# A hybrid decoder layer on one core: output projection by seven products, roots by Ln and Exp, reordered border loads

## The chip, the cores and the metric

The kernel runs on one core of a Trainium2 chip. The core has TensorE (PE: matmuls from SBUF into PSUM), VectorE (DVE), ScalarE (ACT), GpSimd (POOL) and SyncE (SP, which issues the DMAs here). Each takes its instructions in order and waits on semaphores for the others. The metric is device time in microseconds, the median of several executions.

## The reference

One layer over 4096 tokens of width 1024. A norm and one input projection feed three mixers: a chunked gMLP (256 columns), a gated recurrence (256) and eight heads of forgetting attention (512). Their gated outputs y are projected, added to x, and normed again.

```
h = _rmsnorm(x, norm_g[layer])
proj = jnp.einsum('bsd,de->bse', h, w_in[layer])
...
y = jnp.concatenate([y_a, y_b, y_c], axis=-1)
x = x + jnp.einsum('bse,ed->bsd', y, w_out[layer])
...
return _rmsnorm(x, final_norm_g)
```

The norm is x · rsqrt(mean(x²) + 1e-6) · g. All is float32.

## The kernel before

To keep float32's accuracy every large product is made of three: each operand is split into a part that TensorE's fast float32 form holds (`hi`) and the rest (`lo`), and hi·hi, hi·lo and lo·hi are summed in PSUM.

The work comes in three stages. *Projection* (0 to about 1650 us) norms x (`xprep`, `xnorm`), transposes it and makes all columns; the gMLP (`gm_v`) and the recurrence (`hgrn`) run between its products. *Attention* (to 3031 us) walks 32 units, a unit being a pair of heads and a block of 512 queries. For each key tile `do_tile` makes scores `st` and their exponentials `pt`; `do_accs` sums `pt` for the denominators on DVE and POOL; `do_pv` multiplies by the values; `finish_unit` makes the denominators' product `pl`, normalizes and stores to `d_yc`. It is a generator, and `tick(fin)` moves it on by one step. Row maxima of units ahead (`rowmax`, products `sm`, maxima `mp`) run between. A unit's keys (`ka`, `kb`), queries (`qa`, `qb`, `qc`) and values come by DMA in the order in which the program issues them on SP; at the border between the stages `unit_load`, `load_next` and `load_qb` set this order. U0 = 3 units have their maxima made in the projection.

*Output projection* (`out_tile`, from 3031 us) goes over 32 tiles of 128 tokens. A tile has two halves of 512 columns; a half is 8 depth slices × 3 products = 24 matmuls of 128x512 into one PSUM tile `o` (L1588). DVE adds it to the x tile (L1592), ACT squares and sums (L1594); a tick later the root (`rsqrt_small`, L93) and the scaling by the final gain (L1600) follow, and SP stores the tile. `y_load` fetches y for 256 tokens (a block, 16 of them), `y_split` makes hi and lo. The x tiles take three buffers, `qb0` to `qb2`, in turn. w_out is loaded and split during attention (`load_wo`).

`rsqrt_small` makes 1/sqrt on DVE alone, from a bit trick and three Newton steps: 11 operations on 128x1 or 128x4 values, used for all norms.

## Time and profile before

| | us |
|---|---|
| median of 3 runs | 3394.76 (3393.18 to 3395.24) |
| the profiled execution | 3389.97 |
| its span | 3388.1 |
| PE busy | 3264.9 |
| DVE, ACT, POOL busy | 2337.5, 1615.7, 1383.7 |
| output projection, first to last matmul's start | 3031.33 to 3379.40 |

The span is the time from the first to the last instruction of the profiled execution. A row of the table of waits reads "engine, its instruction and line, the engine and instruction that ended the wait: total us, number of waits, the longest". A row of a group reads "line, engine, operation, out<-in, shapes, count | busy us, mean ns | idle time before it and what ended it". A row of the timeline begins with start and duration in us. A matmul's end is modelled, so the distance between starts is its cost.

### The profile page before, as it was taken

The numbers are of one execution on the slowest core, as the hardware profiler recorded it, in microseconds if no ns is written. First come the engines' busy times: TensorE is split into PE (matmuls) and PEld (weight loads), VectorE is DVE, ScalarE is ACT, GpSimd is POOL, SyncE is SP. The second block draws the span as 40 slices with busy tenths as digits, with TensorE's granted clock in tenths as the row PEclk, the third lists the DMA queues.
The fourth block names the chain that finished last, engine by engine and source line by source line (L and its number), as shares of the span: only waits on it lengthen the run. The fifth ranks groups of instructions, "written<-read, shape, count | busy, mean of one in ns | idle before, by whom it ended". The sixth has DMA issues, their size and how long they took to land.

```text
span 3388.1 us, 54808 instructions
## 1 busy us (share of the span) xinstructions
PE 3264.9 (96%) x20314; PEld 2401.5 (71%) x20314; DVE 2337.5 (69%) x4521; ACT 1615.7 (48%) x2979; POOL 1383.7 (41%) x1504
## 2 busy tenths in 40 slices
PE   7999999999999999989899999999999999999999
PEld 7888787978888788777655555555555555558887
DVE  5467745686466845687388888888888888665554
ACT  5435553355434543355255555555555555552221
POOL 2134312342223321344265666666666676660000
PEclk9999999999999999989899999999999999999999
DMA  4432243213342133312550142014201411014443
GB/s 152 138 101 70 70 130 123 94 60 113 114 128 76 51 98 102 104 57 63 123 133 25 35 129 63 26 35 126 66 26 35 116 54 35 27 59 146 148 144 112
DMA packets 204898, 297.06 MB, mean 88 GB/s; under 512 B 19588, under 2 KB 127252, under 8 KB 204630
## 3 DMA queue, kind: packets, MB, share of 16 engines
q1 hardware_dynamic: 204630, 293.56, 28.7%
q8 instruction: 159, 2.61, 0.3%
q14 instruction: 109, 0.89, 0.1%
HBM read 208.83 MB, written 84.43 MB: 87 GB/s over the span
## 4 chain that ended last, share of the span: by engine, by line
PE 53%; DVE 10%; issue 1%; POOL 1%; ACT 1%; DMA 0%; SPq 0%; DVEq 0%; POOLq 0%; ACTq 0%
PE pv L1371 12%; PE o L1588 10%; PE st L1485 7%; PE acc L953 7%; PE sm L149 7%; PE st L1488 6%; DVE mp L162 3%; DVE acc L1354 2%; PE acc L989 2%; PE pl L1311 1%; DVE wlo L249 1%; POOL acc L1354 0%; DVE sm L157 0%; DVE rn L1318 0%; DVE xq L545 0%
## 5 line engine op out<-in xcount | busy, mean ns | idle before, releaser
L1492 ACT ACTIVATE pt<-st,bias 128x512 f32<-128x512 f32 (+3 forms) x1152 | 705.9, 651 | 530.4 <-PE st L1488 431.5
L1354 POOL TENSOR_TENSOR acc<-acc,pt 128x512 f32<-128x512 f32 (+2 forms) x516 | 635.1, 1231 | 316.4 <-PE st L1485 224.4
L162 DVE TENSOR_REDUCE mp<-sm 128x2 f32<-128x1024 f32 (+1 forms) x460 | 536.0, 1192 | 142.9 <-PE sm L149 142.9
L953 PE MATMUL acc<-hhi,whi 128*128 128x512 f32 x1376 | 558.6, 406 | 13.6 <-ACT gu L778 11.1
L953 PE MATMUL acc<-hlo,whi 128*128 128x512 f32 x1376 | 545.3, 396 | 1.3 <-DVE hlo L313 1.3
L953 PE MATMUL acc<-hhi,wlo 128*128 128x512 f32 x1376 | 546.0, 397 | 0.0
L1371 PE MATMUL pv<-pt,v 128*64 128x512 f32 (+3 forms) x2304 | 491.1, 567 | 1.1 <-POOL pt L1497 0.7
L1485 PE MATMUL st<-qa,ka 128*128 128x512 f32 (+2 forms) x1152 | 466.3, 407 | 7.2 <-ACT pt L1492 6.2
L1354 DVE TENSOR_TENSOR acc<-acc,pt 128x512 f32<-128x512 f32 (+2 forms) x516 | 416.2, 807 | 74.8 <-PE pv L1371 34.5
L1488 PE MATMUL st<-qc,kb 68*128 68x512 f32 (+2 forms) x1152 | 441.1, 384 | 3.5 <-DMA qc<-d_m 3.5
L149 PE MATMUL sm<-kb,qb 66*128 66x512 f32 (+2 forms) x1152 | 355.6, 390 | 25.3 <-DVE mp L162 16.1
L1371 PEld LDWEIGHTS pv<-pt,v 128*64 128x64 f32 x2304 | 154.4, 137 | 277.2 <-issue 253.6
L1485 PEld LDWEIGHTS st<-qa,ka 128*128 128x128 f32 x1152 | 219.6, 191 | 179.0 <-issue 96.5
L953 PEld LDWEIGHTS acc<-hhi,whi 128*128 128x128 f32 x1376 | 260.4, 189 | 75.6 <-ACT gu L778 12.5
L249 DVE SCALAR_TENSOR_TENSOR wlo<-wraw,gT,whi 128x256 fp32r<-128x256 f32 (+1 forms) x480 | 255.7, 572 | 75.9 <-ACT whi L248 74.6
L953 PEld LDWEIGHTS acc<-hhi,wlo 128*128 128x128 f32 x1376 | 260.2, 189 | 61.0
L989 PE MATMUL acc<-whi,hhi 128*128 128x256 f32 (+1 forms) x1024 | 295.4, 288 | 7.5 <-ACT FL L996 5.7
L953 PEld LDWEIGHTS acc<-hlo,whi 128*128 128x128 f32 x1376 | 261.0, 190 | 58.0 <-DVE hlo L313 2.3
L989 PE MATMUL acc<-wlo,hhi 128*128 128x256 f32 (+1 forms) x1024 | 289.3, 283 | 0.0
L989 PE MATMUL acc<-whi,hlo 128*128 128x256 f32 (+1 forms) x1024 | 289.1, 282 | 0.0
L149 PEld LDWEIGHTS sm<-kb,qb 66*128 66x128 f32 x1152 | 211.5, 192 | 93.2 <-DVE mp L162 38.2
L1488 PEld LDWEIGHTS st<-qc,kb 68*128 68x128 f32 x1152 | 222.0, 193 | 37.6 <-issue 3.9
(274 smaller groups left out, 4988.4 us busy)
## 6 DMA issues: line engine op xcount, KB each, us to landing
wraw<-in_w_in_dram SPq DMA_DIRECT2D x120, 512.0 KB
x<-in_x_dram SPq DMA_DIRECT2D x88, 512.0 KB
qa<-d_qh SPq DMA_DIRECT2D x64, 256.0 KB
out_dram<-x SPq DMA_DIRECT2D x31, 512.0 KB
kb<-d_kh SPq DMA_DIRECT2D x38, 256.0 KB
d_kh<-chi SPq DMA_DIRECT2D x32, 256.0 KB
d_kl<-clo SPq DMA_DIRECT2D x32, 256.0 KB
d_qh<-chi SPq DMA_DIRECT2D x32, 256.0 KB
```

Source lines behind the costliest of these rows:

```text
L149: nc.tensor.matmul(ps[:, :n], qb[0:66, h, i * P : (i + 1) * P], kb[0:66, h, :n], start=True, stop=True)
L162: nc.vector.tensor_reduce(dst, ps, axis=AX.X, op=ALU.max)
L249: nc.vector.scalar_tensor_tensor(lo[:, k, :n], raw, g, hi[:, k, :n].bitcast(F32), op0=ALU.mult, op1=ALU.subtract)
L953: nc.tensor.matmul(ps, ww[:, k, cs], hh[:, k, :], start=n == 0, stop=n == 3 * KC - 1)
L989: nc.tensor.matmul(o, hh[:, k, ts_], ww[:, k, :width], start=n == 0, stop=n == 3 * KC - 1)
L1311: nc.tensor.matmul(pl[64 * h : 64 * h + 64, :], ones_v, acc[h], start=True, stop=True)
L1354: ins = eng.tensor_tensor(a[:, q0:], src[:, q0:], pts[i][:, q0:], op=ALU.add)
L1371: mm = nc.tensor.matmul(pv[64 * h : 64 * h + 64, q0:], vt[:, i, 64 * h : 64 * h + 64], group[h][i][:, q0:], start=kb == 0, stop=kb == nkb - 1,
L1485: first = nc.tensor.matmul(st[:, qm:], ka_t[g][:, h, cs], qa_t[u % 2][:, h, qm:], start=True, stop=False)
L1488: nc.tensor.matmul(st[:, qm:], kb_t[g][0:68, h, cs], qc_t[u % 2][:, h, qm:], start=False, stop=True)
L1492: nc.scalar.activation(pt[:, q0:], st[:, q0:], AF.Exp, bias=bias_of[u][:, h, kb : kb + 1])
L1588: nc.tensor.matmul(ps, a[:, k % 4, o : o + P], b[k][:, cs], start=n == 0, stop=n == 3 * KC - 1)
```

## The change

**Output projection.** The first NCL = 2 blocks (4 tiles) keep the old form. From block 2 on, `out_block` multiplies the 256 tokens × 1024 by the 1024 × 1024 matrix as 2 × 2 by 2 × 2 blocks with seven products instead of eight. The two token halves and the two depth halves give a11, a12, a21, a22; four combinations s1 to s4 of them are made on POOL (`comb2`). Four combinations of w_out's quarters are made once (`combine`), between the first four tiles, from a second load of w_out. Each of the seven products m0 to m6 is 4 depth slices × 3 = 12 matmuls of 128x512. A product is added by DVE to one or two of the block's four quarters of x; m3 is first added to a copy `u` of m0, which POOL adds to three quarters. m1 and m2 go to the halves of one PSUM tile `ab`, the others to `pr`. While a block is made, the parts (hi by ACT, lo by DVE) for the next ones are made. `norm_out` squares both halves at once.

**Roots.** `rsqrt_small` takes Ln and Exp on ACT and one Newton step on DVE.

**Border.** `load_qb(U0)` is issued before unit 1's loads, and unit 1's entries come first in the list of key tiles to load.

**Denominators.** `finish_unit` moves on twice per eight tiles rather than three times, and waits two yields rather than four before its store.

**w_out.** The raw rows are held for a step, and split by column halves.

```diff
-        nc.vector.tensor_scalar(
-            y.bitcast(I32), v.bitcast(I32), -0.5, 1597463007.0, op0=ALU.mult, op1=ALU.add
-        )
-        for _ in range(3):
-            nc.vector.tensor_tensor(t, y, y, op=ALU.mult)
...
+        nc.scalar.activation(y, ssum, AF.Ln, scale=scale, bias=eps_c)
+        nc.scalar.activation(y, y, AF.Exp, scale=-0.5)
+        nc.vector.tensor_tensor(t, y, y, op=ALU.mult)
+        nc.vector.scalar_tensor_tensor(t, t, -0.5, v, op0=ALU.mult, op1=ALU.mult)
+        nc.vector.scalar_tensor_tensor(y, t, 1.5, y, op0=ALU.add, op1=ALU.mult)
...
-            for _ in range(4):
+            for _ in range(2):
                 yield
             nc.sync.dma_start(d_yc[p][Q], t)
...
         loaded = [0]
+        load_qb(U0)
         if U0 > 1:
             unit_load(1)
             unit_bias(1)
             loaded[0] = 1
+            for e in [e for e in need if e[2] == 1]:
+                need.remove(e)
+                need.appendleft(e)
             while 1 not in ka_t:
                 load_next()
-        load_qb(U0)
...
-                if n in (5, 6, 7):
+                if n in (6, 7):
                     tick(fin)
...
+        def combine(k):
+            raw = [xp.tile([P, D], F32, tag="x", name="wr") for _ in range(2)]
+            for r, kk in zip(raw, (k, k + KH)):
+                nc.sync.dma_start(r, wv[:, kk, :])
+            (b11, b12), (b21, b22) = [(r[:, :512], r[:, 512:]) for r in raw]
...
+            for i, (t, a, b) in enumerate(((t1, b12, b11), (t2, b22, t1), (t3, b22, b12), (t4, b21, t2))):
+                nc.vector.tensor_tensor(t, a, b, op=ALU.subtract)
+                hi, lo = place(4 * k + i)
+                nc.scalar.copy(hi, t)
+                nc.vector.tensor_tensor(lo, t, hi.bitcast(F32), op=ALU.subtract)
...
+            def split(v):
+                pr = big.tile([P, 2, 4, P], F32R, tag="big", name="ya")
+                nc.scalar.copy(pr[:, 0], v)
+                nc.vector.tensor_tensor(pr[:, 1], v, pr[:, 0].bitcast(F32), op=ALU.subtract)
+                parts[t].append(pr)
...
+            plan = [
+                (b11, [x11]), (comb[0], [x12, x22]), (comb[2], [x21, x22]), (comb[1], []),
+                (b22, [x12]), (comb[3], [x21]), (b21, [x11]),
+            ]
+            for m, (b, adds) in enumerate(plan):
+                pr = parts[t][m]
+                ps = ab[:, m - 1] if m in (1, 2) else ps_st.tile([P, 512], F32, tag="st", name="pr")
+                n = 0
+                for k in range(KH):
+                    for i, w in ((0, b[k][0]), (0, b[k][1]), (1, b[k][0])):
+                        nc.tensor.matmul(ps, pr[:, i, k], w, start=n == 0, stop=n == 3 * KH - 1)
+                        n += 1
+                if m == 0:
+                    u = fs.tile([P, 512], F32, tag="rc", name="u", bufs=3)
+                    nc.scalar.copy(u, ps)
+                for xx in adds:
+                    nc.vector.tensor_tensor(xx, ps, xx, op=ALU.add)
+                if m == 3:
+                    nc.vector.tensor_tensor(u, ps, u, op=ALU.add)
+                    for xx in (x22, x21, x12):
+                        nc.gpsimd.tensor_tensor(xx, xx, u, op=ALU.add)
...
+                    xts[t + 1] = [x3_load(2 * t + 2, f"qb{(t + 1 - NCL) % NQB}"), x3_load(2 * t + 3, "")]
```

*DVE in the output stage.* Before, a tile's work is two additions and a root; here from the second scaling of one tile on:

```order
L1600 SCALAR_TENSOR_TENSOR x3_30567<-x3_30567,fry_30719,fgB_29641 128x1024 [waits DVE_49]
L1592 TENSOR_TENSOR x3_30650<-o_30653,x3_30650 128x512 [waits DMAHW5_49,DMAHW4_49,PE_49]
L1592 TENSOR_TENSOR x3_30650<-o_30681,x3_30650 128x512 [waits PE_49]
L1596 TENSOR_TENSOR ss_30652<-ss_30652 128x1 [waits Activation_49]
L99 TENSOR_SCALAR frv_30801<-ss_30652 128x1 [waits DVE_49]
L100 TENSOR_SCALAR fry_30802<-frv_30801 128x1 [waits DVE_49]
L104 TENSOR_TENSOR frt_30803<-fry_30802 128x1 [waits DVE_49]
L105 SCALAR_TENSOR_TENSOR frt_30803<-frt_30803,frv_30801 128x1 [waits DVE_49]
L106 SCALAR_TENSOR_TENSOR fry_30802<-frt_30803,fry_30802 128x1 [waits DVE_49]
```

After, a block in the middle of the stage. x3_30976 is the first tile of its tokens (x11 and x12), x3_30978 the second (x21 and x22); `ya` are lo parts for the blocks ahead; the first row is the last scaling of the block before:

```order
L1624 SCALAR_TENSOR_TENSOR x3_30804<-x3_30804,fry_31116,fgB_29444 128x1024 [waits DVE_49]
L1735 TENSOR_TENSOR x3_30976<-pr_31099,x3_30976 128x512 [waits DMAHW3_49,DMAHW0_49,Activation_49]
L1682 TENSOR_TENSOR ya_31168<-s_31166,ya_31168 128x512 [waits Activation_49]
L1682 TENSOR_TENSOR ya_31190<-s_31188,ya_31190 128x512 [waits PE_49,Activation_49]
L1735 TENSOR_TENSOR x3_30976<-ab_31098,x3_30976 128x512 [waits PE_49]
L1735 TENSOR_TENSOR x3_30978<-ab_31098,x3_30978 128x512
L1682 TENSOR_TENSOR ya_31209<-s_31207,ya_31209 128x512 [waits Activation_49]
L1735 TENSOR_TENSOR x3_30978<-ab_31098,x3_30978 128x512 [waits PE_49]
L1735 TENSOR_TENSOR x3_30978<-ab_31098,x3_30978 128x512 [waits DVE_49]
L1737 TENSOR_TENSOR u_31112<-pr_31171,u_31112 128x512 [waits PE_49]
L1682 TENSOR_TENSOR ya_31247<-yr1_31041,ya_31247 128x512 [waits DMAHW6_49,DMAHW5_49,DMAHW7_49,DMAHW0_49,Activation_49]
L1735 TENSOR_TENSOR x3_30976<-pr_31193,x3_30976 128x512 [waits PE_49,Pool_49]
```

and on to the block's last product and its first root:

```order
L1735 TENSOR_TENSOR x3_30978<-pr_31219,x3_30978 128x512 [waits PE_49]
L1682 TENSOR_TENSOR ya_31317<-s_31315,ya_31317 128x512 [waits Activation_49]
L101 TENSOR_SCALAR frv_31236<-ss_31233 128x1 [waits Activation_49]
L105 TENSOR_TENSOR frt_31238<-fry_31237 128x1 [waits Activation_49]
L106 SCALAR_TENSOR_TENSOR frt_31238<-frt_31238,frv_31236 128x1 [waits DVE_49]
L1735 TENSOR_TENSOR x3_30976<-pr_31250,x3_30976 128x512 [waits PE_49]
L107 SCALAR_TENSOR_TENSOR fry_31237<-frt_31238,fry_31237 128x1 [waits DVE_49]
L1624 SCALAR_TENSOR_TENSOR x3_30978<-x3_30978,fry_31237,fgB_29444 128x1024 [waits DVE_49]
```

The additions of m0 and m1 now stand behind both roots of the block before, m4's behind a wait for POOL, and m6's behind a root's first half, which waits for ACT.

*PE in the output stage.* Before, a tile's first matmul writes a PSUM tile of its own (here the change from one half to the next):

```order
L1588 MATMUL o_30681<-woh_29477,ylo_30547 128x512
L1588 MATMUL o_30737<-woh_29032,yhi_30542 128x512 [waits DVE_49]
L1588 MATMUL o_30737<-wol_29033,yhi_30542 128x512
L1588 MATMUL o_30737<-woh_29032,ylo_30543 128x512
L1588 MATMUL o_30737<-woh_29085,yhi_30542 128x512
```

After, the change from m1 to m2, both in `ab`:

```order
L1729 MATMUL ab_30926<-th_29833,ya_30801 128x512
L1729 MATMUL ab_30926<-tl_29834,ya_30801 128x512
L1729 MATMUL ab_30926<-th_29833,ya_30801 128x512
L1729 MATMUL ab_30926<-th_29552,ya_30824 128x512 [waits DVE_49,Activation_49]
L1729 MATMUL ab_30926<-tl_29553,ya_30824 128x512
L1729 MATMUL ab_30926<-th_29552,ya_30824 128x512
```

The wait for DVE on m2's first row (the last of these) is for the second addition of m1 from the same tile, DVE's row x3_30806<-ab_30926; in the block shown above its like is x3_30978<-ab_31098, ahead of s4's lo part.

*SP at the border.* Before, with `qb` the queries of the next row maxima:

```order
L121 DMA qc_17541<-d_ql_90 64x2x512 [waits DMAHW6_49]
L126 DMA qc_17541<-d_m_130 1x1024 [waits Pool_49]
L126 DMA qc_17541<-d_m_130 1x1024 [waits DMAHW0_49]
L114 DMA kb<-d_kh_66 64x2x512 [waits DMAHW1_49]
L115 DMA kb<-d_cb_114 4x2x512 [waits DMAHW2_49]
L132 DMA ka<-d_kh_66 64x2x512 [waits DMAHW3_49]
L133 DMA ka<-d_kl_74 64x2x512 [waits DMAHW4_49]
L1235 DMA v<-d_v_98 128x4x128 [waits DMAHW5_49]
L1240 DMA qb_17538<-d_qh_84 64x2x512 [waits DMAHW6_49]
L114 DMA kb<-d_kh_67 64x2x512 [waits DMAHW7_49]
```

After:

```order
L1241 DMA qb_17325<-d_qh_84 64x2x512 [waits DMAHW0_49]
L120 DMA qa_17324<-d_qh_82 64x2x512 [waits DMAHW1_49]
L115 DMA kb<-d_kh_68 64x2x512 [waits DMAHW4_49,DMAHW3_49,DMAHW5_49,DMAHW2_49,DMAHW7_49,Activation_49,Pool_49]
L116 DMA kb<-d_cb_116 4x2x512
L115 DMA kb<-d_kh_69 64x2x512
L116 DMA kb<-d_cb_117 4x2x512
L121 DMA qa_17324<-d_qh_82 64x2x512 [waits DMAHW6_49]
L122 DMA qc_17328<-d_ql_90 64x2x512
```

The queries moved from behind unit 1's queries, keys and values to ahead of all of them.

## The prediction

> **What bounds the kernel now.** I read the page first, then PE's waits, then the output stage by itself.

> ```profile
> PE 3264.9 (96%) x20314; PEld 2401.5 (71%) x20314; DVE 2337.5 (69%) x4521; ACT 1615.7 (48%) x2979; POOL 1383.7 (41%) x1504
> 3031.00:3380.00 349.00, 348.79 (x1538) 288.21 (x1536) 175.72 (x498) 76.44 (x157) 3.00 (x3) 1.00 0.38 134
> ...
> PE sm L149 <- DVE mp L162: 16.1, 32, 1.0
> PE acc L953 <- ACT gu L778: 11.1, 6, 3.0
> PE pm L812 <- DVE mp L157: 8.1, 1, 8.1
> PE xtp L306 <- DVE x L291: 8.1, 2, 6.3
> PE sm L149 <- DMA qb<-d_qh: 6.3, 1, 6.3
> PE xtp L306 <- DVE xr1t L105: 6.2, 1, 6.2
> ...
> PE pl L1311 <- DVE acc L1354: 5.9, 4, 2.0
> ...
> PE st L1488 <- DMA qc<-d_m: 3.5, 1, 3.5
> ...
> PE xtp L306 <- DVE xr1t L104: 2.6, 1, 2.6
> ```

> PE is busy for 3264.9 of 3388.1 us, so all its waits together are 123 us, and the time can fall only by fewer products or by some of these small waits. In the output stage (second row) PE is busy for 348.79 of 349 us: nothing else matters there, DVE has half its time free (175.72), ACT more (76.44), and POOL does nothing (3.00). This stage holds the largest edit.

> ```profile
> 3031.33 0.50 PE L1588 MATMUL o<-woh,yhi 128*128 128x512 f32 x1
> ...
> 3379.40 0.39 PE L1588 MATMUL o<-woh,ylo 128*128 128x512 f32 x1
> ...
> L1588 PE MATMUL o<-woh,yhi 128*128 128x512 f32 x512 | 199.3, 389 | 0.0
> L1588 PE MATMUL o<-woh,ylo 128*128 128x512 f32 x512 | 199.2, 389 | 0.0
> L1588 PE MATMUL o<-wol,yhi 128*128 128x512 f32 x512 | 199.2, 389 | 0.0
> ...
> L1592 DVE TENSOR_TENSOR x<-o,x 128x512 f32<-128x512 f32 x64 | 44.1, 690 | 104.8 <-PE o L1588 104.8
> L1600 DVE SCALAR_TENSOR_TENSOR x<-x,fry,fgB 128x1024 f32<-128x1024 f32 (+1 forms) x33 | 41.2, 1252 | 1.1
> ...
> L1564 DVE TENSOR_TENSOR ylo<-yr,yhi 128x1024 fp32r<-128x1024 f32 x29 | 35.5, 1225 | 29.6 <-PE o L1588 27.0 <-ACT yhi L1563 2.6
> ...
> L105 DVE SCALAR_TENSOR_TENSOR frt<-frt,frv 128x1 f32<-128x1 f32 x96 | 15.3, 160 | 3.3
> ...
> L1594 ACT ACTIVATION_READ_ACCUMULATOR junk<-x 128x1 f32 x64 | 11.9, 186 | 0.0
> ```

> The three groups of L1588 have 512 matmuls each, 1536 in all, and begin every (3379.40 − 3031.33)/1535 = 0.2268 us. A tile of 128 tokens has 48 of them, so 256 tokens take 96 × 0.2268 = 21.77 us.

> **The output products.** Four tiles stay as they are: 192 matmuls, 43.5 us. The other 14 blocks of 256 tokens take 7 products of 12 matmuls: 84 × 0.2268 = 19.05 us each, against 21.77. So 14 × 12 = 168 matmuls go, worth 168 × 0.2268 = **38.1 us if PE never waits**. What comes instead lies on DVE, ACT and POOL: per block DVE has nine additions from PSUM at 0.69 (L1592's row), seven lo parts, two final scalings at 1.25 (L1600) and eight small operations at 0.16; POOL has seven additions; ACT seven casts, a copy, two squares and four small functions. On DVE that is some 15 us of 19: by its sum it fits. The order is the trouble. Products m1 and m2 write the two halves of one PSUM tile, `ab`, and the first matmul of m2 waits for DVE's second addition of m1. DVE takes its work in the order of the rows shown with the change, so m2 waits for all that stands ahead of that addition: the last additions and both norms of the block before.

> The trace before has no POOL addition in this stage. The nearest rows are the attention's, where DVE and POOL do the same addition side by side, and the casts of the first stage:

> ```profile
> L1354 POOL TENSOR_TENSOR acc<-acc,pt x516: 448/1286/2146, 1651.5 to 3026.6; 128x512 f32<-128x512 f32 x140, 128x384 f32<-128x384 f32 x24, 128x128 f32<-128x128 f32 x8
> L1354 DVE TENSOR_TENSOR acc<-acc,pt x516: 271/692/1787, 1671.6 to 3030.0; 128x512 f32<-128x512 f32 x140, 128x384 f32<-128x384 f32 x24, 128x128 f32<-128x128 f32 x8
> ...
> L312 ACT CAST hhi<-xtp 128x512 fp32r<-128x512 f32 x64 | 35.6, 586 | 37.0 <-PE xtp L306 37.0
> L265 ACT ACTIVATE junk<-x 128x1024 bf16<-128x1024 f32 x32 | 33.6, 1051 | 5.4 <-DMA x<-in_x_dram 5.4
> ...
> L560 ACT ACTIVATE dec<-z 128x4 f32<-128x4 f32 x16 | 3.3, 206 | 20.4 <-DVE z L471 20.4
> ```

> A POOL addition of 128x512 takes 1.29 us (median). DVE's takes 0.69 by its median and up to 1.79: the same operation is often held up while POOL works. So a lo part (two inputs from SBUF, as this addition) costs 0.69 with POOL quiet and, at a doubling, about 1.35 beside it. [...]

> Now one block, with zero at m2's first matmul and 0.1 us (an estimate, from the 0.04 between the last matmul's modelled end and the addition at 3379.83, plus a start) per step between engines. PE ends m2 at 2.7, m3 at 5.4, m4 at 8.2, m5 at 10.9, m6 at 13.6; the next block's m0 at 16.3 and m1 at 19.05. DVE adds m3 to `u` from 5.5 to 6.2. POOL then adds `u` to three tiles: 3 × 1.29, to 10.2. Only behind the third comes DVE's addition of m4 to x12: 10.3 to 11.0. Two lo parts: 12.4 (13.7 beside POOL). m5's addition: 13.1 (14.4). Square, its read (1.05 + 0.19), Ln and Exp (0.2 each by L560's row): 14.9 (16.3). Two small operations, then m6's addition, which could have begun at 13.7: 16.0 (17.4). First scaling: 17.5 (18.8). The second norm's Square began with the end of m6's addition and its rstd is there at 18.5 (19.9); second scaling: 19.7 (21.2). m0's addition 0.69, two lo parts 1.38, m1's two additions 1.38: 23.2 (24.6). So m2 starts again after **23.3 us with quiet lo parts, 24.7 with contended ones**; I take 24.0, between them, since POOL's four combinations for the next block fall right behind its three adds. Floors: 19.05 if DVE is always in time, 21.7 if the three POOL additions weren't waited for.

> The change of form costs too. Block 2's first x tile is loaded into the buffer that tile 3's output leaves (`qb0`):

> ```profile
> SPq L1579 <- DMA out_dram<-x: 69.0, 29, 3.2
> ```

> Such a load waits up to 3.2 us for the store today, hidden. Counted from the stage's begin, tile 3 ends at 43.5 + about 1.7 (DVE now splits w_out's combinations between the tiles: 8 × 0.69 of extra work per tile ahead of the additions that free PSUM), its norm and issue at 50, the store at 53, the load (512 KB; an estimate of 3.5 to 4 from the store's 3.2) at 57, then five DVE operations of 0.69: block 2's m2 begins at 60.3 where PE alone could at 49. From there 13 steps of 24.0 = 312.0, and the last block's 13.6; the last two blocks prepare no successor, about −3.5. Sum 60.3 + 312.0 + 13.6 − 3.5 = 382.4, against 348.5 before: **+33.9 us**, where the count of matmuls says −38.1.

> **The small edits.** The new root (Ln and Exp on ACT, one Newton step on DVE) takes a chain of 11 small DVE operations to 4 plus 2 on ACT:

> ```profile
> 30.33 0.15 DVE L99 TENSOR_SCALAR xr1v<-xss 128x1 f32<-128x1 f32 x1
> ...
> 34.35 0.75 DVE L291 TENSOR_SCALAR x<-x,rstd 128x1024 f32<-128x1024 f32 x1
> ```

> At the start the last x tile waits 4.0 us in such a chain, of which some 1.1 stay; the transposes that wait for it (6.2 and 2.6 above) come earlier until the next DMA or ACT step binds: −3.0, bounds 0 and −8.8. In the projection the added 0.2 us operations on ACT lie beside PE; the shorter chains may trim the waits of 8.1 (pm) and 11.1 (gu): −2.0, bounds 0 and −8.1. Queries first at the border: PE's 6.3 us on `qb` shrink, but unit 1's loads now stand behind in SP's queue and `qc` (3.5) may be late by as much again: −3.5, bounds −6.3 and +3.5. Denominators a tile later: of 5.9 us on DVE's `acc`, −3.0, bounds 0 and −5.9. w_out's loads and the d_yc store stand beside a busy PE: 0. Sum **−11.5**, bounds −29 and +3.5.

> The tail after the last matmul:

> ```profile
> 3379.83 0.69 DVE L1592 TENSOR_TENSOR x<-o,x 128x512 f32<-128x512 f32 x1 [4.75 <-PE o L1588]
> ...
> 3383.63 1.41 DVE L1600 SCALAR_TENSOR_TENSOR x<-x,fry,fgB 128x512 f32<-128x512 f32 x2
> ```

> DVE's small operations in it get shorter by about 1, the last store is larger again: 0.

> **Sum.** The profiled execution took 3389.97 (span 3388.1 and 1.9 around it), 4.8 below the median of the runs, 3394.76. 3389.97 + 33.9 − 11.5 = 3412.4; on the median's basis 3417.2, which I give as **3417**.

> **Rivals.**
> - *The lock.* Every lo part and small DVE operation that meets POOL waits for its end. The chain from m4's addition to the second scaling then lengthens by about half a POOL addition more, a step of 25.4: 13 × 1.4 = +18, so 3435. For it: the 1.79 us maximum. Against: the median of 0.69 with POOL 41% busy. [...]
> - *Faster by the count.* The wait for `ab` is short because DVE runs ahead: a step of 19.05. It takes 13 × 4.95 = 64 us off and, with block 2 late as above, leaves about 3353; without that, 3345 (−38.1 − 11.5). It decides if DVE gets to m1's additions within 19.05 us of m2's start. Against it: the rows' order, which puts m6 (13.6) ahead of both norms, and from m6's end to m2 at least 7.4 us of DVE against 5.4 of PE.
> - *A small gain.* POOL's three additions don't hold m4's addition: a step of 21.7, 13 × 2.3 = −30: 3387, just faster. It needs POOL additions of under 0.9 us (three from 6.3 on, then m4's addition and two lo parts, all by 11.0); the median row has 1.29.
> - *Only the output edit acts*, and the small ones give nothing: 3429.

> **How the numbers follow.** Forecast (23.3 to 24.7: 3408 to 3426) 0.56, with the last rival 0.10 in the same sign but for its edge; the lock 0.10; the small gain 0.13; the count 0.08; left over, 0.03. A measurement can tell about 0.2% from no change, here 6.8 us. Faster 0.22 (the count, most of the small gain, a little from the rest), same 0.10 (edges of the small gain and of the forecast's low side with the small edits at their best), slower 0.68. The range leaves out the count and little above the lock: 3366 to 3440.

> **What would show it.** Right: in the output stage PE idles some 5 us per block, ended by DVE's x additions, always ahead of m2; DVE's row for the lo parts averages 0.9 to 1.3 us; block starts 24 us apart; one long PE wait near 50 to 60 us after the stage begins. The stage lasts 375 to 400 us and begins about 11 us earlier. Wrong: steps under 21.8, PE waits spread over other products, or a stage that begins later than before.

## The result and the profile after

| | before | after |
|---|---|---|
| median, us | 3393.97 (3389.92 to 3395.24, 4 runs) | 3478.0 (3475.04 to 3480.25, 4 runs) |
| ratio | | 1.0252 (1.0240 to 1.0265) |
| profiled execution, span | 3389.97, 3388.1 | 3478.55, 3476.8 |
| first score product (`st`) begins | 1647.5 | 1641.0 |
| attention, from there to the first `o` | 1383.9 | 1398.2 |
| output stage, first to last matmul's start | 348.1 | 429.1 |

The change is slower by 84 us. I had forecast 3417 and a range to 3440: the sign was right, the size was not. The table, from the timelines of both traces, says where: the projection gains 6.5 us, the attention loses 14.3, and the output stage, with 168 matmuls fewer, takes 81 us more. (The profiled executions differ by 88.6.) In the experiments below, one execution of w_out_only took 11083 us, and its ratio leaves it out. The page of the kernel after:

```profile
PE 3265.4 (94%) x20146; PEld 2396.5 (69%) x20146; DVE 2367.9 (68%) x4144; ACT 1674.3 (48%) x3173; POOL 1536.0 (44%) x1603
```

PE has as much busy time as before, with fewer matmuls. PE's waits, to be read beside those of before:

```profile
PE ab L1729 <- DVE x L1735: 77.8, 14, 11.7
PE sm L150 <- DVE mp L163: 17.0, 35, 1.6
PE pv L1372 <- DVE rn L1319: 15.2, 23, 1.0
PE st L1516 <- ACT pt L1523: 11.0, 6, 6.0
...
PE pm L813 <- POOL gv L803: 7.3, 1, 7.3
...
PE st L1516 <- DMA qa<-d_qh: 5.4, 1, 5.4
```

The wait that I had named is there, in front of `ab` (L1729), 14 times, once per block: 77.8 us (11.7 in block 2, 5.4 in each of the next twelve, 1.5 in the last). That is not yet 81 + 38 = 119 us, the loss and the saving that vanished with it. The windows give the rest. Columns: the stretch and its length in us, busy time of PE, PEld, DVE, ACT and POOL with the count, the granted clock (the share of TensorE's full clock that the profile reports as granted), DMA share and GB/s. The first row is the four tiles of the old form, the last the stage's end, the others blocks:

```profile
3039.00:3087.00 48.00, 45.32 (x191) 36.79 (x191) 40.52 (x60) 18.91 (x38) 11.36 (x8) 0.96 0.60 202
3087.00:3110.00 23.00, 11.32 (x42) 8.85 (x41) 12.73 (x20) 5.32 (x12) 5.02 (x3) 0.70 0.21 70
...
3219.00:3247.00 28.00, 22.62 (x89) 18.14 (x88) 16.05 (x28) 7.71 (x16) 10.51 (x7) 0.88 0.32 113
...
3442.00:3469.00 27.00, 25.27 (x111) 20.27 (x109) 11.42 (x25) 5.53 (x13) 6.13 (x5) 1.00 0.10 39
```

The granted clock is 0.88 in a block, where the stage had 1.00 before; the four old tiles have 0.96 and take 48.3 us instead of 43.5. PE's timeline around one wait (start, duration, then the instruction; idle time before it in brackets):

```profile
3234.31 0.39 PE L1729 MATMUL ab<-tl,ya 128*128 128x512 f32 x1
3234.54 0.39 PE L1729 MATMUL ab<-th,ya 128*128 128x512 f32 x1
3240.30 0.76 PE L1729 MATMUL ab<-th,ya 128*128 128x512 f32 x1 [5.38 <-DVE x L1735]
3240.86 0.63 PE L1729 MATMUL ab<-tl,ya 128*128 128x512 f32 x1
...
3243.43 0.63 PE L1729 MATMUL ab<-tl,ya 128*128 128x512 f32 x1
...
3245.56 0.51 PE L1729 MATMUL pr<-th,ya 128*128 128x512 f32 x1
3245.91 0.39 PE L1729 MATMUL pr<-tl,ya 128*128 128x512 f32 x1
```

m1's last matmul starts at 3234.54, m2's first at 3240.30. Behind the wait of 5.38 us a matmul takes 0.63 us instead of 0.39, and starts lie 0.43 apart instead of 0.227, until 3245.6. So **each such wait is paid twice**: 5.4 us idle, and then 12 matmuls at about half the clock (the profile has 0.50 granted from 3238.96 to 3245.79), which take 5.26 us (3240.30 to 3245.56) in place of 12 × 0.2268 = 2.7, so 2.5 us more. A step is 3245.80 − 3218.54 = 27.3 us in DVE's rows of the same trace:

```profile
3218.54 1.29 DVE L1735 TENSOR_TENSOR x<-ab,x 128x512 f32<-128x512 f32 x2 [5.04 <-PE ab L1729]
3221.35 0.69 DVE L1737 TENSOR_TENSOR u<-pr,u 128x512 f32<-128x512 f32 x1 [1.52 <-PE pr L1729]
3222.00 0.69 DVE L1682 TENSOR_TENSOR ya<-yr,ya 128x512 fp32r<-128x512 f32 x1
3226.37 0.69 DVE L1735 TENSOR_TENSOR x<-pr,x 128x512 f32<-128x512 f32 x1 [3.68 <-POOL x L1739]
...
3229.76 0.68 DVE L1735 TENSOR_TENSOR x<-pr,x 128x512 f32<-128x512 f32 x1
...
3232.83 0.68 DVE L1735 TENSOR_TENSOR x<-pr,x 128x512 f32<-128x512 f32 x1
...
3235.87 1.28 DVE L1624 SCALAR_TENSOR_TENSOR x<-x,fry,fgB 128x1024 f32<-128x1024 f32 x1
3237.07 0.68 DVE L1735 TENSOR_TENSOR x<-pr,x 128x512 f32<-128x512 f32 x1
...
3238.87 1.28 DVE L1735 TENSOR_TENSOR x<-ab,x 128x512 f32<-128x512 f32 x2
...
3245.80 1.29 DVE L1735 TENSOR_TENSOR x<-ab,x 128x512 f32<-128x512 f32 x2 [5.04 <-PE ab L1729]
```

They follow the order that the prediction walked: m3 to `u` at 3221.35, m4's addition only at 3226.37 behind GpSimd, m5's at 3229.76, m6's at 3232.83, the second scaling at 3235.87, m0's at 3237.07, m1's two at 3238.87, done at 3240.15, and PE goes on at 3240.30.

### The profile page after: what moved, and what is told of

The parts are those of the page before. It is cut to its first block, busy times and chain, and to the rows that moved or that the text cites. A ratio compares the mean times of both kernels' runs of the same rounds, so it can differ in the third digit from the quotient of the medians.

```text
span 3476.8 us, 54459 instructions
## 1 busy us (share of the span) xinstructions
PE 3265.4 (94%) x20146; PEld 2396.5 (69%) x20146; DVE 2367.9 (68%) x4144; ACT 1674.3 (48%) x3173; POOL 1536.0 (44%) x1603
## 5 line engine op out<-in xcount | busy, mean ns | idle before, releaser
L1372 PE MATMUL pv<-pt,v 128*64 128x512 f32 (+3 forms) x2304 | 499.2, 573 | 16.2 <-DVE rn L1319 15.2
L1355 DVE TENSOR_TENSOR acc<-acc,pt 128x512 f32<-128x512 f32 (+2 forms) x516 | 418.1, 810 | 80.4 <-PE pv L1372 38.1
L1372 PEld LDWEIGHTS pv<-pt,v 128*64 128x64 f32 x2304 | 162.4, 139 | 294.3 <-issue 249.8
```

What stands on the lines that cost most here:

```text
L1355: ins = eng.tensor_tensor(a[:, q0:], src[:, q0:], pts[i][:, q0:], op=ALU.add)
L1372: mm = nc.tensor.matmul(pv[64 * h : 64 * h + 64, q0:], vt[:, i, 64 * h : 64 * h + 64], group[h][i][:, q0:], start=kb == 0, stop=kb == nkb - 1,
```

## The experiments

Ratios are against the kernel before, run on the same chip, with a 95% interval. The changed kernel's is 1.0252.

**two_psum.** m1 and m2 get a PSUM tile each.

```diff
-            ab = ps_sm.tile([P, 2, 512], F32, tag="sm", name="ab")
+            ab = [ps_sm.tile([P, 512], F32, tag="sm", name="ab") for _ in range(2)]
...
-                ps = ab[:, m - 1] if m in (1, 2) else ...
+                ps = ab[m - 1] if m in (1, 2) else ...
```

> The products m1 and m2 get a PSUM tile each instead of the two halves of one. Theory (m2's wait for m1's additions holds the stage, and PE's clock is halved behind each such wait): the wait of 5.6 us per block in front of m2 goes, m2's matmuls start 0.227 us apart as the others, the block is then bound by DVE's and POOL's chain from one addition of m3 to the next, 20.7 us by the trace of the changed kernel (3221.35 to 3242.0 had m2 been ready), against 27.3: 13 x 6.6 us, together about -85, 3393. Rival (m2 is slow by its operands' places, not by the wait in front of it): the wait goes but m2 still takes 5.3 us: about 3393 + 36 = 3429. Rival (the wait only moves to the PSUM tiles of m5 or m0, with the same DVE order behind it): 3478.

3380.61 us, ratio 0.9977 (0.9967 to 0.9986). PE's waits in the stage of this kernel, and a window of one block:

```profile
PE pr L1729 <- DVE x L1735: 14.0, 13, 1.9
```

```profile
3173.00:3194.00 21.00, 19.90 (x88) 16.15 (x87) 15.24 (x27) 8.30 (x18) 10.99 (x8) 1.00 0.43 151
```

The wait for `ab` is gone, the clock is 1.00, and what is left is 14.0 us in 13 waits, now for the PSUM tile of another product (the last rival's place, at about 1.1 us a block instead of 5.4). The step is 20.4 us and the stage 334.4, against 429.1. The theory gave 3393; the rival of slow operands, 3429, falls: m2 runs at full speed with the same operands.

**fill_wait and fill_half.** Matmuls into a PSUM tile that nobody reads are put between m1 and m2, NW = 24 or 12 of them.

```diff
+        NW = 24
...
+                if m == 1 and t < NSB:
+                    warm = ps_pv.tile([P, 512], F32, tag="pv", name="warm")
+                    for i in range(NW):
+                        nc.tensor.matmul(warm, pr[:, 0, i % 4], b[i % 4][0], start=i == 0, stop=i == NW - 1)
```

> 24 matmuls of 128x512 into a PSUM tile that nobody reads are put between m1 and m2 of each block (5.4 us of work, the length of the wait). Theory (halved clock behind an idle PE): m2's matmuls start 0.227 us apart instead of 0.43, each block falls by about 2.5 us though PE has more to do: 14 x 2.5 = -35, 3443. Rival (m2 is slow by its operands or by DVE at the same PSUM tile): no change, 3478, or slower where the filling goes on past the wait.

> As the filled wait, but with 12 idle matmuls rather than 24 between m1 and m2: PE sits idle for about 2.8 us rather than 0.3 (fill_wait) or 5.5 (the changed kernel). If an idle stretch of 2.8 us doesn't halve PE's clock: 3449 as with 24. If it does: m2's matmuls again 0.43 us apart, 3475 as without. Anything between says that it depends on where the stretch falls.

With 24: 3448.57 us, 1.0181 (1.0166 to 1.0196). With 12: 3460.4 us, 1.0202 (1.0188 to 1.0216). PE does 336 matmuls more than in the changed kernel and the program is 0.7% faster. Two blocks of each, in windows:

```profile
3157.00:3182.00 25.00, 25.00 (x111) 20.44 (x110) 15.58 (x27) 7.72 (x16) 10.50 (x7) 1.00 0.37 128
3182.00:3207.00 25.00, 25.00 (x111) 20.45 (x110) 15.56 (x27) 7.72 (x16) 10.51 (x7) 1.00 0.39 132
```

```profile
3157.00:3182.00 25.00, 23.05 (x94) 18.93 (x95) 13.97 (x25) 7.42 (x16) 10.53 (x7) 0.93 0.34 119
3182.00:3208.00 26.00, 22.68 (x99) 18.14 (x97) 16.59 (x30) 8.02 (x17) 10.50 (x7) 1.00 0.38 128
```

With the wait filled, PE is busy in every microsecond, the clock is 1.00, and the step falls from 27.3 to 24.7: the wait itself, DVE's doing, is as long as before, and only its second price is gone. With half of it filled, an idle stretch of 2.7 us is left in each block shown, and of four blocks in a row, from 3130 to 3233 us, two have a slow m2 behind it (0.93, as in the first window) and two don't (1.00, as in the second). So an idle stretch of that length sometimes halves the clock and sometimes doesn't, and the time lies between. What differs between the two blocks is where the stretch falls. In the trace of the changed kernel the 29 stretches with 0.50 granted begin whole multiples of 3.413 us from one another, to 0.01 us, and so do the 14 in the trace of the kernel before. These are windows of that length around m2 in the same two blocks, the second of them the stretch at 0.50 (PE's busy time stands first, the granted clock behind the last count in brackets):

```profile
3156.85:3160.26 3.41, 1.31 (x6) 1.12 (x7) 2.56 (x5) 0.00 (x0) 0.00 (x0) 1.00 0.93 323
3160.26:3163.68 3.42, 3.42 (x10) 2.68 (x9) 0.33 (x1) 0.00 (x0) 0.00 (x0) 0.50 0.74 266
3180.74:3184.15 3.41, 1.90 (x9) 1.24 (x7) 3.37 (x6) 1.56 (x3) 0.00 (x0) 1.00 0.74 288
3184.15:3187.57 3.42, 2.26 (x10) 1.93 (x11) 1.61 (x3) 0.00 (x0) 0.00 (x0) 1.00 0.92 311
```

In the first block 2.10 us of one window are idle (1.31 are busy), and the next window has half the clock. In the second 1.51 us of the idle stretch fall into one window and 1.16 into the next, and the clock stays full.

**x12_first and u_on_dve.** Which chain makes DVE late? The first puts x12's addition of `u` first on GpSimd, the second gives all three to DVE. m1 and m2 share their PSUM tile in both.

```diff
-                    for xx in (x22, x21, x12):
+                    for xx in (x12, x21, x22):
                         nc.gpsimd.tensor_tensor(xx, xx, u, op=ALU.add)
```

```diff
                     for xx in (x22, x21, x12):
-                        nc.gpsimd.tensor_tensor(xx, xx, u, op=ALU.add)
+                        nc.vector.tensor_tensor(xx, xx, u, op=ALU.add)
```

> The three additions of u on GpSimd in another order, x12, x21, x22 instead of x22, x21, x12; m1 and m2 stay in one PSUM tile. Theory (each block's chain runs through the third GpSimd addition, on which m4's addition to x12 waits): m4's addition begins 2.7 us earlier, m2 waits about 2.8 us instead of 5.5. If PE's clock is halved only behind a wait of more than 3 us or so, the step falls from 27.3 to about 22: -68, 3408. If it is halved behind any such wait: -35, 3441. Rival (the chain does not run through GpSimd): no change, 3476.

3479.18 us, 1.0268 (1.0253 to 1.0284): no gain at all. DVE's timeline in this kernel, in a block that lies 0.9 us later than the one above, and ScalarE's:

```profile
3225.02 0.69 DVE L1735 TENSOR_TENSOR x<-pr,x 128x512 f32<-128x512 f32 x1 [1.47 <-PE pr L1729]
...
3228.13 0.68 DVE L1735 TENSOR_TENSOR x<-pr,x 128x512 f32<-128x512 f32 x1
...
3233.63 0.68 DVE L1735 TENSOR_TENSOR x<-pr,x 128x512 f32<-128x512 f32 x1
```

```profile
3229.39 0.62 ACT L1681 CAST ya<-s 128x512 fp32r<-128x512 f32 x1 [2.23 <-POOL s L1687]
3229.92 1.05 ACT L1619 ACTIVATE junk<-x 128x1024 bf16<-128x1024 f32 x1
```

m3's addition to `u` is at 3222.21 in this block. m4's addition did come early (3225.02: 2.8 us behind m3's, against 5.0 in the changed kernel), and m5's too (3228.13: 5.9 against 8.4). But ScalarE's Square, which needs m5's addition, gained less: ahead of it in ScalarE's order stands the cast of s1, and s1 is made by GpSimd only behind its three additions. Square started at 3229.92, 7.7 us behind m3's addition, against 9.1. The last 1.4 us were lost in the root that follows, in two small operations of DVE that run beside GpSimd's next combinations:

```profile
3231.66 0.79 DVE L105 TENSOR_TENSOR frt<-fry 128x1 f32<-128x1 f32 x1 [0.31 <-ACT fry L104]
3232.49 1.22 DVE L106 SCALAR_TENSOR_TENSOR frt<-frt,frv 128x1 f32<-128x1 f32 x1
```

```profile
3230.70 1.74 POOL L1687 TENSOR_TENSOR s<-yr 128x512 f32<-128x512 f32 x1
3232.40 1.29 POOL L1687 TENSOR_TENSOR s<-yr,s 128x512 f32<-128x512 f32 x1
```

They took 0.79 and 1.22 us, in the changed kernel's block 0.50 and 0.16; with GpSimd quiet each takes 0.16. Each ended within 0.02 us of the end of an addition of GpSimd's (3231.66 + 0.79 = 3232.45 and 3230.70 + 1.74 = 3232.44; 3232.49 + 1.22 = 3233.71 and 3232.40 + 1.29 = 3233.69). In the changed kernel's trace 12 of the operations of L105 meet one; they take 0.49 to 0.51 us, and each ends 0.02 us behind the addition's end. So m6's addition came at 3233.63, 11.4 us behind m3's, as late as ever (11.5). **Behind the addition that was moved forward stood two more waits on GpSimd**: s1's cast, and the small operations of the root.

> The three additions of u on DVE instead of GpSimd; m1 and m2 stay in one PSUM tile. Theory (in x12_first the gain of 1.6 us at m5's addition was lost since ScalarE's cast of s1, ahead of Square, then waited for GpSimd, which makes s1 only behind its three additions; so both chains run through GpSimd): without the three additions there s1 is ready 5 us earlier, DVE's own take 2.1, m6's addition comes some 2 us earlier and m2's wait falls to 3.3: -27 with the halved clock kept, 3448; about -60, 3415, if the clock stays full behind 3.3 us. Rival (GpSimd is not in the chain, DVE's own work is): slower by 13 x 2.1 = 27, 3503.

3476.97 us, 1.0255 (1.0241 to 1.0269): no gain either, and not the rival's loss. DVE's three additions in this kernel:

```profile
3220.04 5.17 DVE L1739 TENSOR_TENSOR x<-x,u 128x512 f32<-128x512 f32 x3
```

They take 5.17 us, 1.72 each, not the 0.69 that I had put in, since GpSimd makes the next block's combinations at that time (three additions of 1.42, 1.62 and 1.74 us between 3219.85 and 3224.67; in the kernel before the 244 additions of 128x512 in L1354 that meet no work of GpSimd's take 0.67 to 0.69 us on DVE). It frees s1 and pays the same on DVE; m2 waits 5.1 or 6.15 us, still with the slow clock behind (in the block shown m2's product is there 5.0 us behind m1's second addition, 3238.36 to 3243.38; its 12 matmuls take 2.7 at full clock). In neither kernel did a shorter wait arise, so they don't tell what a shorter one does to the clock.

**all_mended, best and best_slot.** The two PSUM tiles and the denominators' old steps, with x12 first (all_mended), or with `u` added by DVE (best), and then with block 2's first x tile in the buffer of tile 1 (best_slot):

```diff
-                xts[NCL] = [x3_load(2 * NCL, "qb0"), x3_load(2 * NCL + 1, "")]
+                xts[NCL] = [x3_load(2 * NCL, "qb1"), x3_load(2 * NCL + 1, "")]
...
-                    xts[t + 1] = [x3_load(2 * t + 2, f"qb{(t + 1 - NCL) % NQB}"), ...
+                    xts[t + 1] = [x3_load(2 * t + 2, f"qb{(t + 2 - NCL) % NQB}"), ...
```

> Two PSUM tiles for m1 and m2, x12 first on GpSimd, and the denominators' steps as before, together. Theory: with two PSUM tiles the step of 20.43 us was still DVE's chain behind GpSimd (PE needs 19.05); with x12 first PE sets it: 13 x 1.3 = -17 from 3381; the denominators -6: 3355 to 3360, about 1% under the kernel before. Rival (DVE's own work sets the step): 3375.

3371.91 us, 0.9954 (0.9941 to 0.9966): the rival. PE still waits 12.6 us in 11 waits, for DVE's `u`, and the step is 20.4 as in two_psum.

> Two PSUM tiles, the additions of u on DVE, the denominators' steps as before. Theory: all_mended's step of 20.4 us still ran through GpSimd; without that PE sets it at 19.1: 13 x 1.3 = -17, 3355 (0.9900 of the kernel before). Rival (DVE, now with 17.7 us of work in a block and its waits, sets the step at 20.4 or more): 3372 or above.

3362.32 us, 0.9918 (0.9905 to 0.9932). One block of it:

```profile
3180.00:3199.00 19.00, 19.00 (x85) 15.70 (x84) 17.24 (x31) 8.13 (x17) 5.81 (x4) 1.00 0.49 167
```

PE is busy for all of the 19.0 us and DVE for 17.2: now PE sets the step. What still waits in this kernel's stage, by DVE's waits around block 2:

```profile
DVE x L1735 <- DMA x<-in_x_dram: 3.8, 1, 3.8
```

> As the best so far, with block 2's first x tile in the buffer that tile 1 left rather than tile 3 (and the later blocks' one further). Theory (that load starts only behind tile 3's store, lands 3.8 us late, and PE then runs at the lower clock for some 11 matmuls): -5 to -6, 3357 to 3358 on the scale of 3390 (0.990). Rival (another load or DVE is late there anyway): 0.992.

3354.73 us, 0.9894 (0.9879 to 0.9909). The stage takes 315.0 us (321.7 without), 5 more than 1368 × 0.2268 = 310.3; of its waits only this is left:

```profile
PE o L1636 <- DVE x L1641: 2.7, 1, 2.7
```

It is 1.1% faster than the kernel before, and the best of all.

**old_output, old_ticks.** The changed kernel with one edit undone each.

```diff
-        NCL = min(2, NSB)
+        NCL = NSB
```

```diff
-                if n in (6, 7):
+                if n in (5, 6, 7):
                     tick(fin)
...
-            for _ in range(2):
+            for _ in range(4):
                 yield
```

> The old form of the output projection for all 16 blocks, all else changed (w_out's layout, roots, border, denominators). Theory (the output stage takes 429.5 us against 348.5, the rest of the program 7.9 us more than before): stage back at 348 to 350, 3478 - 80 = 3398, that is 4 us or so above the kernel before (ratio 1.000 to 1.003). Rival (the new layout or roots cost in this stage too): more than 3410.

3395.47 us, 1.0016 (1.0007 to 1.0026), as forecast. All the rest of the change, gains and losses together, costs 0.16%.

> Only the denominators' steps as before (three moves per eight tiles, four yields ahead of the store), all else changed. Theory (the denominators' product, moved one tile later, leaves its PSUM tile so late that the next unit's product with the values waits for DVE: 15.2 us in 23 waits): these waits go, the waits of the denominators for the sums come back (5.9 against 2.1): -11 to -14 us, 3464 to 3467. Rival (attention is longer by its DMAs at the border or by exponentials): no change, 3478.

3470.87 us, 1.0242 (1.0225 to 1.0259). The interval overlaps the changed kernel's, so the ratio alone doesn't show a gain. By the traces the attention takes 1390.8 us, against 1398.2: 7.4 of the 14.3 come from the denominators' steps. The other traces bear that out: with the changed kernel's new steps the attention takes 1396.8 to 1404.4 us in eight traces, with the old ones 1390.8 to 1394.6 in four. It was less than the 11 to 14 that I expected, and it left 6.9 us open.

**root_only, border_only, ticks_only, w_out_only.** The kernel before with one edit alone: the new `rsqrt_small`; the two pieces of the border; the steps of old_ticks the other way; the new `load_wo`, `wo_cost` and `wo_split` with the old products.

> The kernel before with the new root alone (Ln and Exp on ScalarE, one Newton step). Theory (the chains at the start and in the projection get shorter, the rest is hidden): -5 (-2 to -8), 3385; the attention starts 5 us earlier, its length stays. Rival (nothing on the path): no change, 3390.

3382.18 us, 0.9982 (0.9973 to 0.9990), a gain of 6. The attention begins at 1638.0, 9.5 us earlier, and takes 3.5 more.

> The kernel before with the border's load order alone. Theory (the wait of 6.3 us for the row maxima's queries goes, one of 5.4 for unit 1's queries comes in its place): between 0 and -1.5, that is 3389 to 3390, no change that can be told. Rival (the saved wait is kept): -6, 3384.

3387.17 us, 0.9995 (0.9986 to 1.0004): no difference that can be told. PE's waits at its border have, in place of 6.3 for `qb`:

```profile
PE st L1488 <- DMA qa<-d_qh: 5.6, 1, 5.6
```

> The kernel before with the denominators' new steps alone. Theory (the product pl leaves the one PSUM tile that it shares with pv one tile of keys later, so the next pv waits for DVE's rn: 0.66 us in 23 units, 15 us, against 4 to 6 us of the wait for the sums that goes): +6 to +9, 1.002 to 1.0025. Rival (the wait only takes the place of others): 1.000.

3401.14 us, 1.0030 (1.0019 to 1.0042): slower by 10. The wait that it brings, which the kernel before had for 0.3 us:

```profile
PE pv L1371 <- DVE rn L1318: 14.8, 22, 1.0
```

> The kernel before with the new loading and splitting of w_out alone (old output form, old roots, border and denominators). Theory (the attention is 14 us longer in the changed kernel, half of it in its last 100 us, where ScalarE waits with a cast of w_out for a buffer that DVE still reads, exponentials stand behind it, and PE waits and runs on at the lower clock): +7, 1.002 of the kernel before, all of it behind 2980 us. Rival (that wait comes from the other edits' shift in time): 1.000.

3402.09 us, 1.0034 (1.0024 to 1.0045): slower by 11.5. The attention is 10.2 us longer in the trace, and some 8 of that arise between 2981 and 3006 us on the scale of before. ScalarE's waits near the end of its attention, and PE's:

```profile
ACT woh L1423 <- DVE wol L1424: 8.0, 1, 8.0
```

```profile
PE st L1514 <- ACT pt L1521: 10.0, 4, 6.0
```

A cast of w_out sits at the head of ScalarE for 8.0 us, waiting for a lo part that DVE has not come to; the exponentials stand behind it and PE waits 6.0 us in one piece. I had this edit at 0.

**wo_at_once.** The changed kernel, but a row of w_out is split when loaded, not one load later.

```diff
-            if not wo_raw:
-                return 1, 1
...
-            if len(wo_raw) > 1 or k == KC:
+            if wo_raw:
                 wo_split(wo_raw.popleft())
```

> Each row of w_out is split when it is loaded, instead of one load later; all else as changed. Theory (at the attention's end ScalarE's last cast waits 8.0 us for DVE to leave a buffer, exponentials stand behind it, PE waits 6.0 us and runs at a lower clock for a while): this wait goes, the attention's last part is 6 to 8 us shorter, 3468. Rival (the cast then waits for its load instead, or the wait is due to DVE's additions as such): 3476 or more.

3479.25 us, 1.0262 (1.0243 to 1.0281). ScalarE still waits 7.6 us for DVE, now in two pieces, and 3.0 for the loads: holding the row is not the cause. That it is the buffers' rotation under the new layout is argued, not shown.

## Why the prediction was wrong

*The clock behind the wait was left out.* The step that failed is "So m2 starts again after 23.3 us with quiet lo parts, 24.7 with contended ones; I take 24.0". It priced a wait of PE by its length alone: it begins with "PE ends m2 at 2.7, m3 at 5.4", m2 at full pace behind an idle stretch of 5 us. In the block shown m3's addition begins 8.3 us behind m2's first matmul (3213.04 to 3221.35), where the prediction has 5.5. fill_wait shows what 24.0 stood for: with the clock kept at 1.00, m3's addition comes after 5.8 us and the step is 24.7, the figure for contended lo parts. With the clock it is 27.3. Thirteen steps came to 350 us instead of 308.5 (with the −3.5): some 32 of the 41.5 are the clock, the rest is the 0.7 us by which a step without it exceeds 24.0. On the profiled executions the forecast was 3412.4 and the measurement 3478.55. The miss of 66 us is these 41.5, 5.3 before block 2's m2 and 19.5 of the small edits, so the clock is about half of it. The page of before had a hint that I read past: 0.89 granted in its first 45 us, where PE is busy for 25.5. After the change a round has 19 us of work and waits 5.4, and behind the wait starts lie 0.43 us apart, 0.227 without.

*The wait was right.* Its place (m2 behind m1's second addition), its count (14) and nearly its size (5.0 forecast, 5.4 measured) hold, and two_psum shows that it is the cause: with two PSUM tiles the ratio falls from 1.0252 to 0.9977, 93 us. The rivals by which it would not bind (3353, 3387) fall.

*The chain was only half right.* That m4's addition waits for GpSimd's third addition is in the rows (3.68 us idle). That the chain runs through it alone is not. x12_first gained nothing because s1's cast ahead of Square waits for GpSimd as well, and then the root's small operations do; u_on_dve gained nothing because DVE takes the additions at 1.72 us each. From m3's addition to the end of m1's second the chain lasts 18.8 us in the changed kernel and in fill_wait, 18.7 in x12_first, and 18.5 or 19.6 in u_on_dve; by the prediction it was 18.5.

*The lock.* I took lo parts between 0.69 and 1.35. Measured, over all blocks of the changed kernel:

```profile
L1739 POOL TENSOR_TENSOR x<-x,u 128x512 f32<-128x512 f32 x42 | 58.2, 1416 | 237.4 <-DVE u L1737 237.4
...
L1682 DVE TENSOR_TENSOR ya<-s,ya 128x512 fp32r<-128x512 f32 x55 | 43.3, 811 | 0.1
L1682 DVE TENSOR_TENSOR ya<-yr,ya 128x512 fp32r<-128x512 f32 x41 | 40.4, 988 | 8.3 <-ACT ya L1681 8.3
```

That is 0.81 and 0.99 in the mean, and GpSimd's additions take 1.42 in the mean, where I had a median of 1.29. A lo part that meets no work of GpSimd's takes 0.68; the 14 and 39 that do take 1.19 and 1.00 in the mean, up to 1.79. DVE's additions with one input in PSUM take 0.68 to 0.69 with GpSimd at work or without. From 3087 us on 39 lo parts take more than 0.72 us, and each ends 0.55 us behind the end of an addition of GpSimd's; in the kernel before the 90 additions of L1354 on DVE that take so long end alike. Not every small operation is held: 12 of L101, with one input tile, meet work of GpSimd's and take 0.15 us. So what this rival names is at work, in x12_first most plainly, but the step without the clock (24.7) stayed under its 25.4.

*The change of form.* Block 2 was forecast to reach m2 after 60.3 us; it was 65.6. The four tiles ahead took 48.3 where I had 45.2, again a wait (2.7 us for DVE) and the clock behind it (half for 3.4 us). The store that holds up the load was named rightly; best_slot shows it at 6.7 us of the stage, in the kernel where PE sets the step.

*The small edits.* I had −11.5; the changed kernel enters the output stage 8 us later (3039.3 against 3031.3), so the sum was off by 19.5. A stage that begins later than before was one of the prediction's signs of being wrong, and it came. Root: −5 forecast in two places, −6 measured. Border: −3.5 forecast, −1.7 (−4.7 to +1.4) measured: one wait took the other's place. Denominators: −3 forecast, +10 measured: I looked at the wait that goes (`pl` for DVE's sums, 5.9 us before and 2.1 after) and not at who is next behind it, `pv`, which shares `pl`'s only PSUM tile. w_out: 0 forecast, +11.5 measured: I named PE as the cover, but a cast that waits on ScalarE stops the exponentials, and these stop PE. Measured singly the four edits add up to some +14, together in old_output to 5.5: they don't simply add, and why is not shown.

*The range* ended at 3440 since it had no term for the clock behind the wait, and none for a loss from the denominators or w_out.

## What to carry to other kernels

In the changed kernel a wait of TensorE of 5.4 us cost its length and then 2.5 us more at half the clock: in a loop that waits so each round, price both, and fill the wait or shorten it first. When work is taken off the bounding engine, look for the wait that its own buffers bring: two products in one PSUM tile, or two users of a single buffer, tied the engine to its consumer's order here (77.8 us of waits in front of `ab`, 15.2 in front of `pv`). Undoing edits one at a time is worth the runs: of the four small edits here two were plain losses, and with one of them undone, the output's buffers mended and `u` added by DVE, the same idea is 1.1% faster instead of 2.5% slower.

## What the runs showed of the hardware

By waits: those of two_psum, 14.0 us in 13 and 1.9 at most, left the clock at 1.00 in five of six windows of 21 us from 3110 to 3236 us (0.92 in the other); those of 2.7 us in fill_half cost clock in two blocks of four; those of 5.4 us did so in all twelve blocks of `after` that have one. In these twelve the clock was low for two windows, 6.8 us, of which 5.5 lie behind the wait. The steps there, from one m2 to the next, begin at 26.8 us and settle at 27.3, eight windows; whether the clock's windows hold them there is not shown.

*DVE beside GpSimd.* DVE's operations with both inputs in SBUF were held up beside GpSimd's additions, those with an input in PSUM were not (0.68 to 0.69 us either way; 24 of `after` meet such an addition). An addition of two SBUF tiles took 1.72 us in place of 0.69 (u_on_dve), and root operations on 128x1 took 0.79 and 1.22 in place of 0.16, ending with an addition of GpSimd's (x12_first). With m1 and m2 in one PSUM tile, moving the additions of `u` from GpSimd to DVE gave nothing (u_on_dve, 1.0255); with two tiles it gave 0.4% (`best`, 0.9918, against all_mended, 0.9954).
